# A second level of a seven-product scheme inside the first FFN product, for two pairs of neighbouring blocks

## The chip, the core and the metric

The kernel runs on one core of one Trainium2 chip. TensorE (PE) multiplies a stationary 128x128 operand, loaded by a weight load (PEld), with a moving operand and adds into PSUM banks of 128 partitions x 512 fp32; there are eight of them. VectorE (DVE), ScalarE (ACT) and GpSimd (POOL) work beside it, and each runs its own queue in order. SyncE (SP) issues plain loads; loads that add to what lies in the destination are issued by POOL. The metric is the time of one execution in microseconds (us).

## What is computed

The reference is two layers of FFN, mixer, FFN on 512 tokens with 1024 channels, all fp32, and a final norm. The change touches the FFN alone, which occurs four times:

```python
def swiglu(x, w_in, w_out):
    gu = x @ w_in                       # 512 x 1024 by 1024 x 5632
    g, u = jnp.split(gu, 2, axis=-1)    # gate and up, 2816 columns each
    return (jax.nn.silu(g) * u) @ w_out
...
x = x + 0.5 * swiglu(rms_norm(x, ffn1_norm[l]), ffn1_w_in[l], ffn1_w_out[l])
```

`x @ w_in` is the first product of the title, the product with `w_out` the second.

## The kernel before

**Numbers in two parts.** Every fp32 operand is split into a rounded high part and a rest, and a product is three matmuls: high by high, rest by high, high by rest. The stationary operand is a 128x128 tile of the activations, the moving one is 128x512 of the weights. The helper `run` (L367, L368, L370) issues all three.

**The first product.** The first 256 columns of gate and of up are done plainly (`plain`, tile `cl`). The other 2560 columns of each are done in five blocks (`NB = 5`) of 512 gate and 512 up columns. The activations are taken as 2x2 parts (256 tokens by 512 channels), the weights of a block as four parts of 512x512: a and b are the upper and lower channel halves of gate, c and d those of up. One block takes seven products, numbered 1 to 7 in the code, where a plain 2x2 product takes eight. Of the weights, product 1 takes -a, product 2 takes b, 5 takes c+d, 6 takes a+c+d, 3 takes a+b+c+d, 7 takes a+c, 4 takes d. The sums c+a and d+c are made by loads that add (`Raw.load`, L157), the further ones by DVE (`sum`, L191). Product 2 is the lower channel half of the first 256 tokens by b; only gate of those tokens uses it.

A part of the weights comes in two granules of 128x1024 (two channel tiles of 512 columns). Each is one item of a stream in the order in which products use them: load into one of nine `raw` buffers, high part by ACT into `whi` (L196, L198), rest by DVE into `wlo` (L203, L205). There are three `whi` and three `wlo` buffers, so an item is prepared while the two items ahead of it are multiplied, and its buffers come free when the third item back is done. An item of a product is 12 matmuls, a product 24. Up to eight items ahead are loaded.

**PSUM and what follows a product.** Products 1, 6, 7 and 4 go into the pair of banks `A`, 5 and 3 into `B`, 2 into `C`. 6, 7 and 4 add to what is in the banks, so partial sums are copied out between: `snap` (ACT, L601) copies a pair of banks to `sn`, and `less` (DVE, L606) subtracts such a copy from a later state. `gate` (ACT, L705) is the silu, `times` (DVE, L711) multiplies by up. The gated block is transposed by PE (`tr`, L624) in the next block, after that one's first product, and copied by ACT to `at` (L628).

**Order of a block:** 1, 5, 6, 2, 7, 3, 4. `snap` copies banks `A` after 6, product 2 then goes to other banks, and 7 adds to `A`. In the very first FFN's first block 2 comes second. The order of instructions on each engine is set by a scheduler from the program; a stretch at the start and one at the end are kept as written.

**The second product** is done by the same scheme over `at` (tile `o`).

Of the kernel before, what the change touches and what calls it, by code (L numbers as in the profile page):

```python
# [9 lines left out]
F32 = mybir.dt.float32  # L10
F32R = mybir.dt.float32r
# [84 lines left out]
def encoder_kernel(  # L96
# [32 lines left out]
    def pair(s="ps"):  # L129
        return [bank(s), bank(s)]  # L130
# [86 lines left out]
    def stage_items():  # L217
        items, st = [], 0

        def add(*a, **k):  # L220
            items.append(Item(*a, stage=st, **k))

        made = {}

        def strassen(s, name, idx, sizes, order, dma=False):
            r = made.setdefault((s, name("a"), idx), {}) if dma and len(order) < 7 and order[0] > 2 else {}
            for q, q2 in () if r else (("a", ""), ("b", ""), ("c", "a"), ("d", "c")):
                r[q] = [
                    Raw((s, name(q), idx, g), n, *[(s, name(z), idx, g) for z in q2]) for g, n in enumerate(sizes)
                ]  # L230
# [4 lines left out]
            for m in order:  # L235
                for g in range(len(sizes)):
                    a, b, c, d = [r[q][g] for q in "abcd"]
                    if m == 1:
                        add(a, neg=True)
                    elif m == 2:  # L240
                        add(b)
                    elif m == 3:
                        add(r["s"][g] if "s" in r else d, None if dma else b)
                    elif m == 4:
                        add(d2[g])
                    elif m == 5:
                        add(d, then=a.key if dma and order is not ORDER_W else None)
                    elif m == 6:
                        t = r["s"][g] if "s" in r else d
                        add(t, None if dma else a, then=b.key if dma else None)  # L250
                    else:
                        add(c)

        def out_sizes(c):
            return (1024, 512) if c == 0 else (1024, 1024)

        def ffn(s):
            first = not items
            for g in range(4):
                add(Raw((s, "cl", g)), parts=2 if first and g < 2 else 1, pieces=2 if first and g == 0 else 1)  # L260
            for j in range(NB):
                order = (1, 2, 5, 6, 7, 3, 4) if s == (0, 1) and j == 0 else (1, 5, 6, 2, 7, 3, 4)
                strassen(s, lambda q: q, j, (1024, 1024), order)
            for order in ((1,), (2,), (5, 6, 7, 3), (4,)):
                for c in range(3):
                    strassen(s, lambda q: "o" + q, c, out_sizes(c), order)

        for l in range(L):
            ffn((l, 1))
            st += 1  # L270
            s = (l, 0)
            two = (1024, 1024)
            for g in VG:
                add(Raw((s, "v", g)), kept=g == VG[0])
            for g in range(3):
                add(Raw((s, "up", g), UC * len(UK[g]), (s, "uq", g)))
            for g in range(2):
                add(Raw((s, "un", g)), minus=(s, "um", g))
            for g in range(8):
                add(Raw((s, "qk", g)))  # L280
            for i in range(2):
                add(Raw((s, "fp", i), 1024, (s, "fq", i)))
                add(Raw((s, "fq", i)), minus=(s, "fp", i))
            for i in range(2):
                strassen(s, lambda q: "g" + q, i, two, ORDER_0[0 : 2 - i], True)
            for g in range(2):
                add(Raw((s, "n", 0, g)))
            for i, order in ((0, (5,)), (1, (2,)), (0, (6,)), (1, (5,)), (0, (7, 3)), (1, (6,)), (0, (4,)), (1, (7, 4, 3))):
                strassen(s, lambda q: "g" + q, i, two, order, True)
# [3 lines left out]
            strassen(s, lambda q: "w" + q, 0, two, ORDER_W, True)  # L293
            ffn((l, 2))
        return items

# [75 lines left out]
    def split(hi, lo, src, scale=None):  # L372
        if scale is None:
            S.activation(hi, src, AF.Copy)
            return V.tensor_tensor(lo, src, hi.bitcast(F32), ALU.subtract)
        S.activation(hi, src, AF.Copy, scale=scale)
        return V.scalar_tensor_tensor(lo, src, scale, hi.bitcast(F32), ALU.mult, ALU.subtract)
# [220 lines left out]
    def snap(ps):  # L598
        t = slot(F32, "sn", (2, T))
        for b in range(2):  # L600
            S.activation(t[:, b, :], ps[b], AF.Copy)  # L601
        return t
# [5 lines left out]
    def stage_ffn(norm, nxt, late):  # L608
# [52 lines left out]
        first = norm.idx == 0  # L661
        if not first:
            norm.rstd()
        with tc.manual_schedule(engines={mybir.EngineType.DVE, mybir.EngineType.Activation}) if first else nullcontext():
            t1 = combo(b11, b11, b12, ALU.subtract, "t1")
            if first:
                norm.squares(0, 0)
            t3 = combo(b12, b12, b22, ALU.subtract, "t3")
            if first:
                norm.squares(0, 1)  # L670
            t2 = combo(b22, b22, b11, ALU.add, "t2")
            if first:
                norm.squares(1, 0)
            if first:
                ws.prep(ws.pos + 3)
            V.tensor_tensor(b21, b21, b22, ALU.subtract)
            t4 = (hx[0][:, :, 256:512], lx[0][:, :, 256:512])
            split(t4[0], t4[1], b21)
# [87 lines left out]
        def second(s1):  # L766
            pc = pair("C")
            product(pc, acts[2], K4, True)
            less(pc, s1)

        for jb in range(NB):
            f0 = 2 + 4 * jb
            if first and jb == 0:
                with tc.manual_schedule(engines={mybir.EngineType.DVE, mybir.EngineType.Activation}):
                    pa = pair("A")
# [1256 lines left out]
```

## Time and profile before

| | us |
|---|---|
| median of three runs (1870.36 to 1871.58) | 1871.33 |
| the profiled execution | 1870.75 |
| its span, first to last instruction | 1869.0 |
| PE busy | 1859.4 |
| DVE busy | 1492.2 |
| ACT busy | 1175.9 |
| POOL busy | 182.8 |

A row of a group or a timeline names line, engine, operation, output<-input and shape; in brackets or behind a bar stands how long the engine was idle before it and what it waited for. Matmuls overlap: each has a duration of its own, but the next starts before it ends, so the distance between starts is what a matmul takes of PE. The granted TensorE clock is 0.999 of full speed over the span.

### The profile page before, as it was taken

How to read it: one execution, taken by the hardware profiler on the slowest of the kernel's cores; microseconds unless marked ns; L12 is line 12 of the kernel's file. 1: busy time of each engine (PE TensorE's matmuls, PEld its weight loads, DVE VectorE, ACT ScalarE, POOL GpSimd, SP SyncE). 2: the span in 40 equal slices, each digit the busy share in tenths (PEclk: the TensorE clock that was granted, in tenths of full speed). 3: DMA queues.
4: the chain of work that ended last, by engine and by line, in shares of the span. 5: the costliest groups of instructions: out<-in, count | busy, mean ns of one | idle time of the engine just before them, and what ended most of it. 6: DMA issues, size and time to landing. Idle time of an engine off the chain costs nothing.

```text
span 1869.0 us, 25963 instructions
## 1 busy us (share of the span) xinstructions
PE 1859.4 (99%) x9609; PEld 1584.6 (85%) x9609; DVE 1492.2 (80%) x1831; ACT 1175.9 (63%) x1751; POOL 182.8 (10%) x219
## 2 busy tenths in 40 slices
PE   9999999999999999999999999999999999999998
PEld 7888888889998888888888888888899988888886
DVE  7777799758879777779977777997687797777898
ACT  6655565768656655566665556667676576555665
POOL 0101011100211001001000000101002110100010
PEclk9999999999999999999999999999999999999999
DMA  8777588864998477659757764979649985766595
GB/s 296 205 193 202 150 239 267 243 209 126 245 258 224 131 201 193 181 150 266 240 148 188 208 178 153 253 230 281 202 132 252 247 222 140 196 181 168 179 270 184
DMA packets 110319, 384.57 MB, mean 206 GB/s; under 512 B 12512, under 2 KB 12640, under 8 KB 110192
## 3 DMA queue, kind: packets, MB, share of 16 engines
q1 hardware_dynamic: 79952, 276.81, 42.1%
q0 software_dynamic: 29808, 105.32, 30.7%
q8 instruction: 75, 1.23, 0.3%
q10 hardware_dynamic: 432, 0.79, 0.1%
q14 instruction: 52, 0.43, 0.1%
HBM read 375.13 MB, written 6.29 MB: 204 GB/s over the span
## 4 chain that ended last, share of the span: by engine, by line
PE 97%; DVE 1%; ACT 0%; DMA 0%; issue 0%; DVEq 0%; ACTq 0%
PE A L367 9%; PE A L370 9%; PE A L368 9%; PE o L370 7%; PE o L367 7%; PE o L368 7%; PE B L367 5%; PE B L368 5%; PE B L370 5%; PE ps L367 3%; PE ps L368 3%; PE ps L370 3%; PE C L370 2%; PE C L368 2%; PE C L367 2%; PE tr L624 2%
## 5 line engine op out<-in xcount | busy, mean ns | idle before, releaser
L205 DVE TENSOR_TENSOR wlo<-raw,whi 128x1024 fp32r<-128x1024 f32 (+2 forms) x524 | 619.4, 1189 | 224.4 <-ACT whi L198 221.5
L198 ACT ACTIVATE whi<-raw 128x1024 fp32r<-128x1024 f32 (+2 forms) x524 | 537.5, 1032 | 341.6 <-PE A L368 134.1
L157 POOL DMA_DIRECT2D raw<-in_wst_dram x170 | 147.5, 871 | 1449.2 <-DMA raw<-in_wst_dram 826.1
L191 DVE TENSOR_TENSOR raw<-raw,raw 128x1024 f32<-128x1024 f32 (+1 forms) x128 | 151.4, 1188 | 2.4
L367 PE MATMUL A<-whi,xh 128*128 128x512 f32 x320 | 124.5, 389 | 0.0
L368 PE MATMUL A<-whi,xl 128*128 128x512 f32 x320 | 124.5, 389 | 0.0
L705 ACT ACTIVATE th<-sn,r 128x512 f32<-128x512 f32 x80 | 57.0, 715 | 73.7 <-DVE sn L606 73.7
L196 ACT ACTIVATE whi<-raw 128x1024 fp32r<-128x1024 f32 x76 | 78.7, 1036 | 35.3 <-issue 17.1
L203 DVE SCALAR_TENSOR_TENSOR wlo<-raw,whi 128x1024 fp32r<-128x1024 f32 x76 | 90.6, 1192 | 8.9 <-ACT whi L196 8.8
L370 PE MATMUL A<-wlo,xh 128*128 128x512 f32 x320 | 92.1, 389 | 0.0
L601 ACT ACTIVATE sn<-A 128x512 f32<-128x512 f32 x96 | 56.1, 590 | 45.9 <-PE A L370 45.9
L368 PEld LDWEIGHTS A<-whi,xl 128*128 128x128 f32 x320 | 60.1, 188 | 12.5
L370 PEld LDWEIGHTS A<-wlo,xh 128*128 128x128 f32 x320 | 60.1, 188 | 12.5
L367 PEld LDWEIGHTS A<-whi,xh 128*128 128x128 f32 x320 | 60.1, 188 | 12.5
L367 PE MATMUL B<-whi,t1h 128*128 128x512 f32 x160 | 63.7, 398 | 0.0
L367 PE MATMUL A<-whi,t2h 128*128 128x512 f32 x160 | 62.5, 391 | 0.0
L367 PE MATMUL B<-whi,xh 128*128 128x512 f32 x160 | 62.4, 390 | 0.0
L368 PE MATMUL B<-whi,xl 128*128 128x512 f32 x160 | 62.3, 390 | 0.0
L368 PE MATMUL B<-whi,t1l 128*128 128x512 f32 x160 | 62.3, 390 | 0.0
L368 PE MATMUL A<-whi,t2l 128*128 128x512 f32 x160 | 62.3, 389 | 0.0
L368 PE MATMUL A<-whi,t3l 128*128 128x512 f32 x160 | 62.2, 389 | 0.0
L367 PE MATMUL C<-whi,xh 128*128 128x512 f32 x160 | 62.2, 389 | 0.0
(454 smaller groups left out, 4897.5 us busy)
## 6 DMA issues: line engine op xcount, KB each, us to landing
raw<-in_wst_dram SPq DMA_DIRECT2D x463, 512.0 KB
raw<-in_wst_dram POOLq DMA_DIRECT2D x184, 512.0 KB, 8.0
raw<-in_wst_dram SPq DMA_DIRECT2D x28, 256.0 KB
vc<-vd SPq DMA_DIRECT2D x28, 256.0 KB
bm<-in_near_dram SPq DMA_DIRECT2D x16, 384.0 KB
vd<-v SPq DMA_DIRECT2D x8, 512.0 KB
dft<-in_dft_dram POOLq DMA_DIRECT2D x4, 514.0 KB, 10.0
x<-in_xin_dram SPq DMA_DIRECT2D x4, 512.0 KB
```

The source lines that it names most:

```text
L157: z = G.dma_start(out=self.t, in_=wst[GRAN_AT[plus]][:, 0 : self.n], accum_op=ALU.add)
L191: V.tensor_tensor(self.raw.t, self.raw.t, self.add.t, ALU.add)
L196: S.activation(self.out[0][:, cs], self.raw.t[:, cs], AF.Copy, scale=-1.0)
L198: S.activation(self.out[0][:, cs], self.raw.t[:, cs], AF.Copy)
L203: self.last = V.scalar_tensor_tensor(lo, t, -1.0, hi.bitcast(F32), ALU.mult, ALU.subtract)
L205: self.last = V.tensor_tensor(lo, t, hi.bitcast(F32), ALU.subtract)
L367: PE.matmul(ps, lh, rh, start=start, stop=False, skip_group_check=again)
L368: PE.matmul(ps, *((lh, rl) if w == "l" else (ll, rh)), start=False, stop=False, skip_group_check=again)
L370: PE.matmul(ps, *((ll, rh) if w == "l" else (lh, rl)), start=False, stop=stop, skip_group_check=again)
L601: S.activation(t[:, b, :], ps[b], AF.Copy)
L624: PE.transpose(tr[:, k, b * P : (b + 1) * P], a[:, b, (q + k) * P : (q + k + 1) * P], ident)
L705: S.activation(th[:, b, :], g[:, b, :], AF.Silu, scale=norm.r[:, c : c + 1])
```

## The change

Blocks 1 and 2, and blocks 3 and 4, are made pairs. Product 2 of both blocks of a pair has the same activations (256 tokens by 512 channels); their weights, b of the one and b of the other side by side, are 512 x 1024. This joined product is now done by the seven-product scheme once more, with parts of 128 tokens by 256 channels and 256 x 512. An inner part of the weights is then just one granule, and an inner product is one item and six matmuls (two channel tiles, three matmuls each, one bank). Block 0 keeps its product 2.

- `stage_items`: seven inner items take the place of the four items of two products 2. In the first block of a pair inner 1, 5, 2, 6 and 3 stand ahead of the outer products 5, 6, 7, 3 and 4; in the second block inner 7 and 4 stand ahead of 6 and 7. The inner weights are loaded apart from b of the outer product 3, which was shared with product 2 before and is now loaded for the sum of product 3 alone. Two of the inner items need a load that adds, two need a sum on DVE.
- `inner_parts` and `inner_split` make the inner activations once per FFN: four DVE operations of 128x256, and a split of 128x1024 on ACT and DVE. Three of the seven inner activations are slices of what is there.
- `pair_block` replaces the block's body: one bank `qA` lives through the pair, `qB` and `qC` through its first block; results are added into `s1` piece by piece, with one copy `sq` by ACT in the first block.

```diff
+ORDER_P = (1, 5, 6, 7, 3, 4)
+INNER = (((5, 1), (6, 5), (7, 2), (3, 6), (4, 3)), ((6, 7), (7, 4)))
+PAIRS = (1, 3)
...
             for j in range(NB):
-                order = (1, 2, 5, 6, 7, 3, 4) if s == (0, 1) and j == 0 else (1, 5, 6, 2, 7, 3, 4)
-                strassen(s, lambda q: q, j, (1024, 1024), order)
+                if not j:
+                    four(s, lambda q: q, j, (1024, 1024), ORDER_0 if first else ORDER_W)
+                    continue
+                if j in PAIRS:
+                    key = [[(s, "b", j + z, g) for g in range(2)] for z in range(2)]
+                    a, b, c = Raw(key[0][0]), Raw(key[0][1]), Raw(key[1][0], 1024, key[0][0])
+                    d, d2 = Raw(key[1][1], 1024, key[1][0]), Raw(key[1][1])
+                    parts = {1: (a, None, True), 2: (b,), 3: (d, b), 4: (d2,), 5: (d,), 6: (d, a), 7: (c,)}
+                inner = dict(INNER[j not in PAIRS])
+                for m in strassen(s, lambda q: q, j, (1024, 1024), ORDER_P):
+                    if m in inner:
+                        add(*parts[inner[m]])
...
+        def inner_parts(src):
+            y = [[src[:, 2 * i : 2 * i + 2, b * P : (b + 1) * P] for b in range(2)] for i in range(2)]
+            t = slot(F32, "v", (4, 2, P))
+            v = [t[:, z] for z in range(4)]
+            V.tensor_tensor(v[0], y[0][0], y[0][1], ALU.subtract)
...
+        def inner(ps, m, begin):
+            wh, wl = ws.next()
+            h, l = fine[m]
+            terms = []
+            for k in range(2):
+                z = slice(k * T, (k + 1) * T)
+                terms.append((ps, h[:, k], l[:, k], wh[:, z], wl[:, z], "r", begin and k == 0, k == 1))
+            run(terms, not begin)
...
+        def pair_block(jb, late_at):
+            one = jb in PAIRS
+            pa = pair("A")
+            product(pa, acts[1], K4, True)
+            s1 = snap(pa)
+            settle_at()
+            if one:
+                qa = kept["a"] = bank("qA")
+                inner(qa, 1, True)
+                V.tensor_tensor(s1[:, 0, :], qa, s1[:, 0, :], ALU.add)
...
+            product(pa, acts[6], K4, False, again=True)
+            s2 = snap(pa)
+            if one:
+                qc = bank("qC")
+                inner(qc, 2, True)
+                V.tensor_tensor(s1[:, 0, :], qc, s1[:, 0, :], ALU.subtract)
+            else:
+                inner(qa, 4, False)
+                V.tensor_tensor(s1[:, 0, :], qa, s1[:, 0, :], ALU.subtract)
+                z1 = gate(s1, 0)
+            product(pa, acts[7], K4, False, again=True)
...
+                if jb == 1:
+                    inner_split()
+                pair_block(jb, late_at)
```

Summed over the program, PE has 48 matmuls of 128x512 fewer (9620 to 9572). DVE has 24 `wlo` and 16 sums of 128x1024 more, 24 operations of 128x512 that read or finish an inner product more than it had for `C`, 16 of 128x256 and 4 splits. ACT has 24 `whi`, 8 copies `sq` and 4 splits more. SP issues 40 loads of 512 KB more, POOL 16 adding loads.

Three places, all in the first FFN's block 1. In these rows lines of the changed kernel are some 20 to 50 higher for the same code (L601 is L620, L606 is L625, L198 is L201, L205 is L208, L191 is L194); numbers behind a name only tell buffers apart.

ACT after product 6, before:

```order
L198 ACTIVATE whi_811<-raw_645 128x1024
L601 ACTIVATE sn_827<-A_684 128x512
L198 ACTIVATE whi_834<-raw_663 128x1024
L601 ACTIVATE sn_827<-A_685 128x512
L198 ACTIVATE whi_853<-raw_686 128x1024
L705 ACTIVATE th_872<-sn_722,r_515 128x512
```

ACT at the same place now:

```order
L201 ACTIVATE whi_832<-raw_669 128x1024
L842 ACTIVATE sq_828<-qB_817 128x512
L201 ACTIVATE whi_850<-raw_695 128x1024
L620 ACTIVATE sn_866<-A_693 128x512
L201 ACTIVATE whi_872<-raw_714 128x1024
L620 ACTIVATE sn_866<-A_694 128x512
L201 ACTIVATE whi_886<-raw_611 128x1024
```

The two copies of `A` and the `whi` between them keep their order; the copy `sq` comes ahead of them, and the silu of the first half moves to the block's end.

DVE from the items of product 6 to those of product 7, before:

```order
L205 TENSOR_TENSOR wlo_754<-raw_558,whi_753 128x1024
L191 TENSOR_TENSOR raw_558<-raw_558,raw_620 128x1024
L205 TENSOR_TENSOR wlo_773<-raw_566,whi_772 128x1024
L191 TENSOR_TENSOR raw_566<-raw_566,raw_645 128x1024
L205 TENSOR_TENSOR wlo_794<-raw_620,whi_793 128x1024
L205 TENSOR_TENSOR wlo_812<-raw_645,whi_811 128x1024
L205 TENSOR_TENSOR wlo_835<-raw_663,whi_834 128x1024
L205 TENSOR_TENSOR wlo_854<-raw_686,whi_853 128x1024
```

DVE from the end of inner 1 (`qA`) to product 7 now:

```order
L833 TENSOR_TENSOR sn_733<-qA_762,sn_733 128x512
L208 TENSOR_TENSOR wlo_779<-raw_611,whi_778 128x1024
L194 TENSOR_TENSOR raw_611<-raw_611,raw_563 128x1024
L208 TENSOR_TENSOR wlo_798<-raw_570,whi_797 128x1024
L194 TENSOR_TENSOR raw_570<-raw_570,raw_776 128x1024
L208 TENSOR_TENSOR wlo_819<-raw_590,whi_818 128x1024
L194 TENSOR_TENSOR raw_590<-raw_590,raw_795 128x1024
L208 TENSOR_TENSOR wlo_833<-raw_669,whi_832 128x1024
L208 TENSOR_TENSOR wlo_851<-raw_695,whi_850 128x1024
L208 TENSOR_TENSOR wlo_873<-raw_714,whi_872 128x1024
```

The sums for product 3 (`raw_776` and `raw_795` are b) still stand right behind the items of product 6; the sum for inner 6 (`raw_611`) and one inner item come between, and the sums now wait for a load of b that was there before for product 2.

PE where product 6 ends, before (the last two matmuls of 6, then product 2; its 24 matmuls run on to product 7):

```order
L370 MATMUL A_685<-wlo_773,t2h_336 128x512 x2
L367 MATMUL C_830<-whi_793,xh_136 128x512
L368 MATMUL C_830<-whi_793,xl_137 128x512
L367 MATMUL C_830<-whi_793,xh_136 128x512
L368 MATMUL C_830<-whi_793,xl_137 128x512
L367 MATMUL C_831<-whi_793,xh_136 128x512
```

PE there now (the last two of 6, the whole of inner 2, the first of 7):

```order
L389 MATMUL A_694<-wlo_819,t2h_336 128x512 x2
L386 MATMUL qC_869<-whi_832,xh_136 128x512
L387 MATMUL qC_869<-whi_832,xl_137 128x512
L386 MATMUL qC_869<-whi_832,xh_136 128x512
L387 MATMUL qC_869<-whi_832,xl_137 128x512
L389 MATMUL qC_869<-wlo_833,xh_136 128x512 x2
L386 MATMUL A_693<-whi_850,t3h_327 128x512
```

Between the last matmul of 6 into `A` and the first of 7 into the same banks there were 24 matmuls into `C`; now there are 6 into `qC` (or, in the second block of a pair, into `qA`).

More of the change, by code (lines that the diff above doesn't have):

```diff
@@ L252, in strassen, with four @@
                         add(c)
+        def four(*a):
+            for _ in strassen(*a):
+                pass
         def out_sizes(c):
@@ L284, in stage_items @@
             for i in range(2):
-                strassen(s, lambda q: "g" + q, i, two, ORDER_0[0 : 2 - i], True)
+                four(s, lambda q: "g" + q, i, two, ORDER_0[0 : 2 - i], True)
             for g in range(2):
@@ L288, in stage_items @@
             for i, order in ((0, (5,)), (1, (2,)), (0, (6,)), (1, (5,)), (0, (7, 3)), (1, (6,)), (0, (4,)), (1, (7, 4, 3))):
-                strassen(s, lambda q: "g" + q, i, two, order, True)
+                four(s, lambda q: "g" + q, i, two, order, True)
                 st += not i and order[0] == 5
@@ L292, in stage_items @@
                 add(Raw((s, "n", 1, g)))
-            strassen(s, lambda q: "w" + q, 0, two, ORDER_W, True)
+            four(s, lambda q: "w" + q, 0, two, ORDER_W, True)
             ffn((l, 2))
```

54 lines of the change are left out of this document (53 added, 1 removed).

## The prediction, made before the changed kernel was run

> **What bounds the kernel now.** I read the busy shares first, then the chain of waits.
>
> ```profile
> span 1869.0 us, 25963 instructions
> ...
> PE 1859.4 (99%) x9609; PEld 1584.6 (85%) x9609; DVE 1492.2 (80%) x1831; ACT 1175.9 (63%) x1751; POOL 182.8 (10%) x219
> ...
> PE 97%; DVE 1%; ACT 0%; DMA 0%; issue 0%; DVEq 0%; ACTq 0%
> ```
>
> PE is busy all but 9.6 us and makes 97% of the chain that ended last. A share is a mean over stages, so I asked for the stages that the change touches: the first FFN's blocks 2 and 3 (from one transpose of gated results to the next, see the third fence), and its second product.
>
> ```profile
> 108.90:148.80 39.90, 39.90 (x186) 33.28 (x185) 28.40 (x28) 22.56 (x29) 3.46 (x4) 1.00 0.68 183
> 148.80:188.60 39.80, 39.80 (x185) 33.19 (x184) 28.42 (x28) 22.60 (x31) 3.46 (x4) 1.00 0.70 184
> 234.00:326.00 92.00, 92.00 (x409) 76.20 (x408) 89.87 (x95) 57.18 (x71) 11.30 (x14) 1.00 0.85 252
> ```
>
> Behind the stretch and its length stand PE, PEld, DVE, ACT and POOL busy, the granted clock, the DMA share and GB/s. In a block PE never stops, DVE works 28.4 of 39.9 us and ACT 22.6. In the second product DVE is at 89.87 of 92 us, and PE still doesn't stop. So a matmul taken away shortens the kernel, as long as preparation, copies and loads keep up.
>
> **The matmuls.** The price is the distance of starts. From the timeline of PE, product 2 of block 2 and what follows, and from the chain, the transposes in blocks 2 and 3:
>
> ```profile
> 126.84 0.39 PE L367 MATMUL C<-whi,xh 128*128 128x512 f32 x1
> ...
> 132.28 0.39 PE L367 MATMUL A<-whi,t3h 128*128 128x512 f32 x1
> ```
>
> ```profile
> 114.36 1.75 PE tr L624 x16
> ...
> 154.21 1.75 PE tr L624 x16
> ```
>
> 24 matmuls take 132.28 - 126.84 = 5.44 us, 0.2267 each (the 0.39 is a latency that overlaps). A block is 7 x 5.44 + 1.75 = 39.83 us, and the transposes stand 39.85 apart: nothing else is in it. A pair now has 2 x 24 = 48 matmuls in products 2, and would have 7 x 6 = 42. Six fewer in 2 pairs x 4 FFNs make 48 x 0.2267 = **10.88 us**. The first block of a pair becomes 174 matmuls and 16 transposes, 41.2 us, the second 156, 37.1 us: 78.3 where two blocks take 79.7. [...] The trace's 0.2267 us, which fills the block to 0.02 us, decides here.
>
> **DVE and ACT.** Groups over block 2, and the 128x256 group of the whole run:
>
> ```profile
> L205 DVE TENSOR_TENSOR wlo<-raw,whi 128x1024 fp32r<-128x1024 f32 x12 | 14.7, 1225 | 9.1 <-ACT whi L198 9.1
> L198 ACT ACTIVATE whi<-raw 128x1024 fp32r<-128x1024 f32 x13 | 13.8, 1061 | 11.8 <-PE A L368 9.0 <-PE B L368 1.5 <-PE C L368 0.7
> ...
> L191 DVE TENSOR_TENSOR raw<-raw,raw 128x1024 f32<-128x1024 f32 x4 | 4.9, 1225 | 0.1
> ...
> L705 ACT ACTIVATE th<-sn,r 128x512 f32<-128x512 f32 x4 | 2.9, 716 | 4.1 <-DVE sn L606 4.1
> ...
> L601 ACT ACTIVATE sn<-A 128x512 f32<-128x512 f32 x4 | 2.4, 589 | 2.4 <-PE A L370 2.4
> ...
> L606 DVE TENSOR_TENSOR sn<-A,sn 128x512 f32<-128x512 f32 x2 | 1.4, 688 | 0.6 <-PE A L370 0.6
> ```
>
> ```profile
> L427 DVE TENSOR_SCALAR xr<-xt,xt 128x256 f32<-128x256 f32 x14 | 4.3, 349 | 0.0
> ```
>
> DVE waits for ACT, and ACT for PE to free a `whi` buffer: preparation is held back by PE, not the other way. Per pair DVE gets three more `wlo` (3 x 1.225), two sums (2 x 1.225) and three operations on 128x512 (seven for the inner products less four on `C`, 3 x 0.69): 8.2 us, beside 56.8 us of now, 65.0 of 78.3 us (83%). The first block bears most: three items, two sums, two on 128x512, 7.5 us, 35.9 of 41.2 us (87%). The second has the same count of items and one 0.69 more, 29.1 of 37.1 us. ACT gets 3 x 1.061 + 0.589 = 3.8 us per pair, 49 of 78.3. All of it lies beside PE. An inner item is only 1.36 us of matmuls against 1.225 of `wlo`, or 2.45 with a sum. But inner items stand singly between two granules of 2.72 us, and the sums run early, in DVE's gaps. Going through DVE's order of the first block with these durations and the three buffers (a `wlo` not before the third item back is done), each `wlo` ends some 2 us or more ahead of the matmul that reads it, the tightest in product 4 of the first block. I take 0 for it. A missed cover would show as PE waiting for `wlo`.
>
> The inner activations: four operations of 128x256 at 0.35 (the nearest row; up to 0.69, the row of twice the width), 1.4 us, in DVE's queue ahead of the last activation split at each FFN's start; and once 1.2 us on DVE and 1.06 on ACT in block 1. In the second FFN's start:
>
> ```profile
> 621.87 1.22 DVE L676 TENSOR_TENSOR xr<-xr,xr 128x1024 f32<-128x1024 f32 x1
> ...
> 624.27 1.23 DVE L375 TENSOR_TENSOR xl<-xr,xh 128x1024 fp32r<-128x1024 f32 x1 [1.19 <-ACT xh L374]
> ...
> 626.45 1.23 DVE L203 SCALAR_TENSOR_TENSOR wlo<-raw,whi 128x1024 fp32r<-128x1024 f32 x1 [0.95 <-ACT whi L196]
> ```
>
> ```profile
> 628.33 0.39 PE L367 MATMUL A<-whi,xh 128*128 128x512 f32 x1
> ```
>
> The queue has gaps of 1.19 and 0.95 us behind the insertion, and the `wlo` at 626.45 is the second granule of a product that starts at 628.33: needed at 628.33 + 2.72 + 0.91 = 632.0, ready 4.3 us earlier. 1.4 to 2.8 us late costs nothing there.
>
> **The copy ahead of product 7.** Product 7 writes banks that ACT still copies. Product 2's 5.44 us covered that; now an inner product's 1.36 us does. After product 6 of block 2, which ends at 126.84, ACT has:
>
> ```profile
> 125.68 0.60 ACT L601 ACTIVATE sn<-A 128x512 f32<-128x512 f32 x1 [1.21 <-PE A L370]
> 126.59 1.06 ACT L198 ACTIVATE whi<-raw 128x1024 fp32r<-128x1024 f32 x1 [0.31 <-PE A L368]
> 127.56 0.58 ACT L601 ACTIVATE sn<-A 128x512 f32<-128x512 f32 x1
> ```
>
> The second copy ends at 128.14, 1.30 us after product 6. Product 7's first four matmuls go to the first bank, so the second is touched 1.36 + 0.91 = 2.27 us after: 0.97 us in hand. In a pair's second block a silu half stands between the first copy and that `whi`, 0.72 us, of which 0.40 fall on ACT's idle 0.31 and the overlap: the copy is done some 0.3 us later, with 0.6 in hand. I take 0; the place comes 2 x 8 = 16 times.
>
> **The loads.** Over blocks 2 and 3 (79.7 us, 20 plain loads and 8 adding):
>
> ```profile
> q1 hardware_dynamic: 2880, 10.49, 38.6%
> q0 software_dynamic: 1113, 4.08, 29.9%
> ...
> raw<-in_wst_dram POOLq DMA_DIRECT2D x8, 512.0 KB, 7.9
> ```
>
> A plain load takes 0.386 x 79.7 / 20 = 1.54 us of all engines, an adding one 2.98. A pair will have 25 and 10: 68.3 of 78.3 us, 87%, where the second product lives with 85% and 252 GB/s. So the sum of bandwidth fits (234 GB/s). In order: SP issues a load when its buffer comes free. The shortest lead is b of product 3, whose buffer the sum for product 6 frees and whose own sum stands seven DVE operations later: six of about 1.15 us (their starts) and one of 0.69, 7.6 us. No row has a plain load's landing. The adding one's 7.9 us bounds it from above; 0.52 MB at the stretch's 184 GB/s, 2.8 us, is nearer, since a plain load occupies the engines half as long. Even at 7.9 DVE would wait 0.3 us, and the `wlo` behind it has 3.6 us in hand. 0.
>
> **Sum.** 10.88 us, nothing on the other side. The profiled execution of 1870.75 becomes 1859.9; the median stands 0.58 above that execution, so **1860.5** is what I forecast.
>
> **Rivals.** (1) *Slower: ACT loses the race ahead of product 7.* For it: cover falls from 5.44 to 1.36 us and ACT's queue is in order, so a `whi` that waits for its buffer or a silu that waits for DVE (4.1 us of such idle in the group above) holds the copy. Against it: 0.6 to 0.97 us in hand, and the silu that stands ahead is of the half that is ready earlier. Each us beyond that stops PE 16 times; at 0.68 us (1.3 to 1.65 late in all) the gain is gone. Late by two more ACT operations of 1.06, 2.1 less 0.8 in hand, it costs 21 us: about 1881. (2) *DVE falls behind in the first block of a pair.* For it: 87%, and waits now take 11 of 40 us, of which only 5.3 are left. Against it: those waits are for PE's buffers and shrink when DVE is late. If 0.7 us per pair are missing, 5.6 us come back: 1866. (3) *The loads of b come late.* For it: 87% of DMA, with adding loads between. Against it: 7.6 us of lead and 3.6 in hand. [...] Were DVE to stop 5 us in each first block, 1.4 would reach PE, 8 times: 11 us, so no change. (4) *The gain is real but given back in the second product,* since DVE, 98% busy there, may set that stage's end: arriving 2.72 us earlier in each FFN would then only make PE wait, about 1871. Against it: DVE enters that stage without arrears, for in block 4, which ends at 228.4,
>
> ```profile
> 220.52 1.23 DVE L205 TENSOR_TENSOR wlo<-raw,whi 128x1024 fp32r<-128x1024 f32 x1 [0.99 <-ACT whi L198]
> ```
>
> it still waits, and the changed block 4 leaves it some 7 us free.
>
> **Chances and range.** As forecast, 1859 to 1862: 0.78. Part of it lost by (2) or a smaller (1), 1862 to 1867: 0.08. No change by (3) or (4): 0.05. Slower by (1) or several of these: 0.09. A difference under 0.2% (3.7 us) can't be told from none here. Faster by more is the first and most of the second, 0.85; same 0.06; slower 0.09. Below, nothing but the noise of runs (0.6 us each way) adds to the removed matmuls; above, I go to 1866, where (2) ends.
>
> **What would show it.** PE 48 matmuls fewer; the transposes of a pair about 41.2 and 37.1 us apart; no idle time of PE ahead of `A`, `qA`, `qB`, `qC`; the second product starting 2.72 us earlier in each FFN. DVE busy 1492.2 + 8 x 8.2 + 4 x 2.6 = 1568, 84%; 56 loads, 29.4 MB more. Wrong would be PE waiting for `sn` by ACT (1), for `wlo` (2), DVE's sums waiting for `raw` (3), or PE idle in `o` (4).

## The result

The changed kernel takes 1859.76 us (1858.98 to 1860.66), the kernel before beside it 1871.45 (1870.36 to 1872.14): a ratio of 0.9938, 95% interval 0.9921 to 0.9955. The forecast was 1860.5 in a range of 1859 to 1866, and the likeliest case came in.

From the page of the changed kernel, the lines that answer to those shown of before:

```profile
span 1857.9 us, 26118 instructions
...
PE 1847.8 (99%) x9561; PEld 1574.3 (85%) x9561; DVE 1556.5 (84%) x1915; ACT 1203.1 (65%) x1787; POOL 196.8 (11%) x235
...
DMA packets 118384, 413.94 MB, mean 223 GB/s; under 512 B 13408, under 2 KB 13536, under 8 KB 118256
```

PE has 9561 matmuls instead of 9609, 48 fewer, and is busy 11.6 us less; the span is 11.1 us shorter. PE is idle 10.1 us, where it was 9.6. The chain of waits in the first FFN has the transposes that close each block of columns:

```profile
73.74 1.75 PE tr L643 x16
...
114.94 1.75 PE tr L643 x16
...
152.07 1.75 PE tr L643 x16
```

They stand 41.20 and 37.13 us apart: the first block of a pair and its second block. Both numbers were forecast. Busy times between them (stretch and length, then PE, PEld, DVE, ACT, POOL, the granted clock, DMA share and GB/s), for both blocks of the first pair and the first block of the second:

```profile
69.40:110.60 41.20, 41.20 (x192) 34.35 (x191) 36.52 (x38) 25.74 (x32) 4.33 (x5) 1.00 0.78 219
110.60:147.70 37.10, 37.10 (x174) 30.96 (x173) 28.54 (x30) 22.18 (x28) 4.32 (x5) 1.00 0.88 248
147.70:188.90 41.20, 41.20 (x192) 34.35 (x191) 35.08 (x36) 25.86 (x34) 4.06 (x6) 1.00 0.80 220
```

PE never stops in them. DVE is at 36.5 and 35.1 of 41.2 us in the first blocks. The race ahead of product 7 is in the timeline of ACT (`sn` of L620 is the second bank's copy), first in a first block, then in a second one:

```profile
88.68 1.06 ACT L201 ACTIVATE whi<-raw 128x1024 fp32r<-128x1024 f32 x1 [0.31 <-PE A L387]
89.65 0.58 ACT L620 ACTIVATE sn<-A 128x512 f32<-128x512 f32 x1
...
128.12 0.71 ACT L755 ACTIVATE th<-sn,r 128x512 f32<-128x512 f32 x1
128.73 1.05 ACT L201 ACTIVATE whi<-raw 128x1024 fp32r<-128x1024 f32 x1
129.68 0.59 ACT L620 ACTIVATE sn<-A 128x512 f32<-128x512 f32 x1
```

and PE's first matmuls of product 7 on the second bank in the two blocks:

```profile
91.20 0.39 PE L386 MATMUL A<-whi,t3h 128*128 128x512 f32 x1
...
131.05 0.39 PE L386 MATMUL A<-whi,t3h 128*128 128x512 f32 x1
```

The copies end at 90.23 and 130.27, so 0.97 and 0.78 us are in hand.

**Where the time went, by FFN.** From the start of the last `cl` row of PE's timeline (two matmuls) to that of the first `o` matmul lie the five blocks, and all kernels below are set beside each other so. The kernel before was run again beside each set of kernels, with medians from 1870.19 to 1871.45 us; each ratio is to the one beside it:

| kernel (label of its run) | FFN 1 | FFN 2 | FFN 3 | FFN 4 | median us | ratio to before, 95% interval |
|---|---|---|---|---|---|---|
| before | 198.92 | 198.82 | 198.82 | 198.83 | 1871.45 | |
| after | 196.40 | 196.11 | 196.10 | 196.11 | 1859.76 | 0.9938 (0.9921 to 0.9955) |
| e1_one_pair | 197.76 | 197.46 | 197.46 | 197.47 | 1866.04 | 0.9976 (0.9966 to 0.9986) |
| e2_six_back | 199.08 | 198.82 | 198.83 | 198.82 | 1870.29 | 0.9998 (0.9989 to 1.0007) |
| e6_last_only | 198.98 | 198.83 | 198.83 | 196.11 | 1868.66 | 0.9992 (0.9983 to 1.0000) |
| e6_first_three | 196.40 | 196.11 | 196.11 | 198.82 | 1862.70 | 0.9958 (0.9945 to 0.9970) |
| e8_no_cover | 199.08 | 198.84 | 198.84 | 198.84 | 1871.82 | 1.0005 (0.9996 to 1.0013) |
| e8_wlo_first | 196.76 | 196.48 | 196.49 | 196.49 | 1861.28 | 0.9950 (0.9938 to 0.9963) |
| e3_copy_plus1 | 199.36 | 199.06 | 199.25 | 199.10 | 1871.50 | 1.0009 (1.0000 to 1.0018) |
| e3_copy_plus3 | 205.53 | 205.23 | 208.45 | 206.88 | 1907.69 | 1.0207 (1.0193 to 1.0221) |
| e3_copy_in_four | 196.39 | 196.11 | 196.10 | 196.10 | 1860.29 | 0.9946 (0.9933 to 0.9960) |
| e4_dve_plus4 | 196.67 | 196.72 | 196.11 | 196.11 | 1860.43 | 0.9948 (0.9935 to 0.9960) |
| e4_dve_plus8 | 204.80 | 205.26 | 201.93 | 202.02 | 1891.08 | 1.0111 (1.0098 to 1.0125) |
| e9_loads_plus4 | 196.40 | 196.11 | 196.11 | 196.11 | 1860.73 | 0.9946 (0.9934 to 0.9959) |

Of the 11.1 us of span, 10.65 lie in these stretches (2.52 + 3 x 2.71). In the first FFN 0.20 us are missing in block 0 and the first product of block 1, which the change leaves alone: from the last `cl` row to the chain's first transposes it takes 45.34 us there instead of 45.14. Most of that, 0.17, lies beside PE's early transposes, which the new schedule has in other places. The rest of the span's difference is outside of the stretches: 1.0 us less up to the first FFN's last `cl` row, 1.0 more behind the last FFN's first `o`, and half a us less between the first two FFNs. The lengths at the two ends differ by as much between the kernels below, also where nothing in them is changed (see the last FFN, below), and I don't count them as the change's.

### The profile page after: what moved, and what is told of

It reads as the page before. It is cut to its first block, busy times and chain, and to the rows that moved or that the text cites. A ratio compares the mean times of both kernels' runs of the same rounds, so it can differ in the third digit from the quotient of the medians.

```text
span 1857.9 us, 26118 instructions
## 1 busy us (share of the span) xinstructions
PE 1847.8 (99%) x9561; PEld 1574.3 (85%) x9561; DVE 1556.5 (84%) x1915; ACT 1203.1 (65%) x1787; POOL 196.8 (11%) x235
## 2 busy tenths in 40 slices
DMA packets 118384, 413.94 MB, mean 223 GB/s; under 512 B 13408, under 2 KB 13536, under 8 KB 118256
## 3 DMA queue, kind: packets, MB, share of 16 engines
q8 instruction: 75, 1.23, 0.3%
## 4 chain that ended last, share of the span: by engine, by line
PE 97%; DMA 1%; DVE 1%; issue 0%; ACT 0%; POOL 0%; ACTq 0%; DVEq 0%; SPq 0%; POOLq 0%
PE A L386 9%; PE A L389 9%; PE A L387 9%; PE o L389 7%; PE o L386 7%; PE o L387 7%; PE B L386 5%; PE B L387 5%; PE B L389 5%; PE ps L386 3%; PE ps L387 3%; PE ps L389 3%; PE tr L643 2%; PE cl L387 2%; PE cl L389 2%; PE cl L386 2%
## 5 line engine op out<-in xcount | busy, mean ns | idle before, releaser
L208 DVE TENSOR_TENSOR wlo<-raw,whi 128x1024 fp32r<-128x1024 f32 (+1 forms) x540 | 638.7, 1191 | 170.3 <-ACT whi L201 169.3
L201 ACT ACTIVATE whi<-raw 128x1024 fp32r<-128x1024 f32 (+1 forms) x540 | 555.2, 1034 | 317.8 <-PE A L387 89.7
L160 POOL DMA_DIRECT2D raw<-in_wst_dram x186 | 161.4, 873 | 1458.9 <-DMA raw<-in_wst_dram 766.5
L194 DVE TENSOR_TENSOR raw<-raw,raw 128x1024 f32<-128x1024 f32 (+1 forms) x144 | 171.2, 1193 | 2.7
L199 ACT ACTIVATE whi<-raw 128x1024 fp32r<-128x1024 f32 x84 | 87.1, 1037 | 42.1 <-issue 21.5
L206 DVE SCALAR_TENSOR_TENSOR wlo<-raw,whi 128x1024 fp32r<-128x1024 f32 x84 | 99.8, 1196 | 4.6 <-ACT whi L199 4.5
L620 ACT ACTIVATE sn<-A 128x512 f32<-128x512 f32 x96 | 56.2, 591 | 46.4 <-PE A L389 46.4
L386 PE MATMUL A<-whi,t3h 128*128 128x512 f32 x160 | 62.2, 389 | 0.0
```

Source lines behind the costliest of these rows:

```text
L160: z = G.dma_start(out=self.t, in_=wst[GRAN_AT[plus]][:, 0 : self.n], accum_op=ALU.add)
L194: V.tensor_tensor(self.raw.t, self.raw.t, self.add.t, ALU.add)
L199: S.activation(self.out[0][:, cs], self.raw.t[:, cs], AF.Copy, scale=-1.0)
L201: S.activation(self.out[0][:, cs], self.raw.t[:, cs], AF.Copy)
L206: self.last = V.scalar_tensor_tensor(lo, t, -1.0, hi.bitcast(F32), ALU.mult, ALU.subtract)
L208: self.last = V.tensor_tensor(lo, t, hi.bitcast(F32), ALU.subtract)
```

## The experiments

The theory is the prediction's: PE sets the time, a matmul costs its distance of starts, and preparation, copies and loads have something in hand. The rivals are its four.

**Half of the change.** One pair instead of two:

```diff
-PAIRS = (1, 3)
+PAIRS = (1,)
...
-                if not j:
+                if j not in (1, 2):
...
-            if jb:
+            if jb in (1, 2):
```

> Only blocks 1 and 2 are joined; blocks 3 and 4 are done as in the kernel before. Theory (PE sets the time, a matmul costs 0.2267 us, all else is covered): 24 of the 48 matmuls are back, 5.44 us, so the change of 11.69 us becomes some 6.2 us: 1871.45 - 5.44 = 1866.0, and 1865.2 if the measured 1859.76 + 5.44 is taken. Rival: the gain comes from somewhere else (an earlier start, other order of DVE's or ACT's work at the start of a FFN, where the four operations for the inner activations stand): then one pair would bring all of it, 1860, or none, 1871. The transposes of blocks 1 and 2 stand 41.2 and 37.1 us apart, those of blocks 3 and 4 39.85.

Measured 1866.04 us. Each of the last three FFNs gained 1.36 us, half of 2.71. Its chain of waits in the first FFN:

```profile
73.87 1.75 PE tr L643 x16
...
115.07 1.75 PE tr L643 x16
...
152.20 1.75 PE tr L643 x16
...
192.05 1.75 PE tr L643 x16
```

41.20, 37.13 and, for block 3 as it was, 39.85 us. The gain lies in the pairs, in proportion to their number, and nothing of it comes from the FFN's start, where the inner activations are made in this kernel too. (In this kernel and in e6_last_only the blocks of the first FFN that are no longer joined take the weights of products 2, 5 and 6 in another order than their code multiplies them, so their values are others; matmuls, loads and copies are as many.)

**The six matmuls given back.** The inner product into `qB` is done twice:

```diff
+            if m == 5:
+                run(terms, not begin)
             run(terms, not begin)
```

> Each pair does its inner product into qB twice, with the same weights: 6 matmuls more per pair, 48 in the kernel, and nothing else changed. Theory: 48 x 0.2267 = 10.88 us come back, 1859.76 + 10.88 = 1870.6, as the kernel before; the first block of a pair becomes 42.56 us. [...] If DVE, ACT or the loads set the pace in the pairs, the added PE work would be covered: 1860.

Measured 1870.29, no different from before, and 10.5 us above the changed kernel. In the chain:

```profile
73.71 1.75 PE tr L643 x16
...
116.27 1.75 PE tr L643 x16
...
153.40 1.75 PE tr L643 x16
```

The first block is 42.56 us, 1.36 more than with six matmuls fewer: 0.227 each. All else of the change is still in this kernel, its DVE operations, sums, copies and loads, and it costs nothing: FFNs 2 to 4 take 198.82 us as before, and the first 0.16 more, which are those of block 0 told above.

**Rival (4), the second product.** The change in the last FFN alone, and in all but the last:

```diff
-                if not j:
+                if not j or s != (1, 2):
...
-            if jb:
+            if jb and late:
```

> Only the last FFN joins products 2; the three others are as before. Theory: 12 matmuls fewer, 2.72 us: 1871.45 - 2.72 = 1868.7. Rival (4) for this one FFN: its second product gives 1.1 us back, as the profile after shows there (PE waits for wlo), so the change brings 1.6 us: 1869.8. In the profile: from the last matmul of the closing block of columns to the first of the second product 195.9 us instead of 198.6, and in the second product PE idle for 1.1 us or not.

> Only the first three FFNs join products 2, the last is as before. Theory: 36 matmuls fewer, 8.16 us: 1870.55 - 8.16 = 1862.4. Rival (4) in the last FFN's second product (there the change gives 1.1 us back): the three bring 8.2 and the fourth only 1.6, so this kernel would be only 1.6 us above the changed one, 1861.4. In the profile: from the first matmul of the last second product to the end 114.2 us, as before, where the changed kernel has 115.2; if it is 115 to 116 here too, with the last FFN unchanged, this length varies by execution and the change doesn't set it.

Measured 1868.66 and 1862.70. The first is 1.9 to 2.8 us below before, depending on which median of it is taken (1870.55 beside this run, 1871.45 beside the changed kernel), the second 7.5 to 8.8 (1870.21 and 1871.45). The stretches are sharper: 2.71 to 2.72 us where a FFN is changed (2.52 in the first), at most 0.06 elsewhere. For the first three FFNs rival (4) is settled by PE's starts. Counted from the first `o` matmul, the first 400 of some 460 starts of each second product agree with those of the kernel before to 0.002 us, in every kernel of the table. For the last FFN the end of the span has to do. What lies behind the last FFN's first `o` matmul, of the kernel before, the changed one, e6_last_only and e6_first_three:

```profile
1754.82:1869.00 114.18, 106.82 (x479) 88.15 (x477) 106.45 (x129) 69.95 (x91) 13.07 (x15) 0.99 0.77 226
```

```profile
1742.69:1857.90 115.21, 107.56 (x479) 88.00 (x477) 106.72 (x129) 70.21 (x91) 13.10 (x15) 0.99 0.78 223
```

```profile
1750.82:1867.10 116.28, 107.52 (x479) 88.00 (x477) 106.72 (x129) 69.96 (x91) 13.04 (x15) 0.98 0.76 222
```

```profile
1746.65:1861.90 115.25, 107.25 (x479) 88.14 (x477) 106.69 (x129) 69.93 (x91) 13.04 (x15) 0.98 0.77 224
```

The kernel whose last FFN is unchanged has 115.25 us here, as the changed one, against 114.18 of before. The length varies by 2.1 us between the profiled kernels, and not with the arrival: e8_no_cover (below), which comes to this place as late as before, has 116.3, and e2_six_back, as late, 115.1. In the changed kernel PE waits there once for `wlo`, 0.27 us, a sign that the prediction had named for (4); but e2_six_back has the same wait of 0.26. So this us is not given back by an earlier arrival, and rival (4) falls. What makes the length vary stays open.

**Rival (1), the cover ahead of product 7.** First the cover is taken away: the inner product between products 6 and 7 goes behind 7, with PE's order held.

```diff
-INNER = (((5, 1), (6, 5), (7, 2), (3, 6), (4, 3)), ((6, 7), (7, 4)))
+INNER = (((5, 1), (6, 5), (3, 2), (13, 6), (4, 3)), ((6, 7), (3, 4)))
...
-                    if m in inner:
-                        add(*parts[inner[m]])
+                    for q in (m, 10 + m):
+                        if q in inner:
+                            add(*parts[inner[q]])
...
+            fixed = tc.manual_schedule(engines={mybir.EngineType.PE})
+            fixed.__enter__()
             pa = pair("A")
...
+            product(pa, acts[7], K4, False, again=True)
+            less(pa, sb)
             if one:
                 qc = bank("qC")
                 inner(qc, 2, True)
...
-            product(pa, acts[7], K4, False, again=True)
-            less(pa, sb)
...
+            fixed.__exit__(None, None, None)
             times(z1, pa, 0)
```

> The inner product that stands between product 6 and product 7 (qC in a pair's first block, qA in the second) is moved behind product 7, PE's order otherwise held as it was: product 7 follows product 6 at once. Theory (the copy of the second bank ends 1.30 us after product 6, product 7 touches that bank after its first four matmuls, 0.91 us): PE stops 0.39 us at 16 places, 6.2 us, 1866.0, with PE waiting for sn by ACT; the silu that stood ahead of the copy in the second block stands later too, so both blocks lose the same. Rival: the copy is fast enough or the wait is caught up elsewhere, 1859.8. Rival the other way: ACT falls behind for good, over 1870.

Measured 1871.82: the whole gain is gone, 12 us where 6.2 were expected. The waits of PE, and then its timeline in a first block (the fourth matmul of product 7 and the fifth, which goes to the second bank) and in a second one:

```profile
PE A L387 <- ACT sn L621: 5.9, 16, 0.5
```

```profile
89.51 0.39 PE L388 MATMUL A<-whi,t3l 128*128 128x512 f32 x1
90.17 0.50 PE L387 MATMUL A<-whi,t3h 128*128 128x512 f32 x1 [0.27 <-ACT sn L621]
90.51 0.40 PE L388 MATMUL A<-whi,t3l 128*128 128x512 f32 x1
...
129.92 0.39 PE L388 MATMUL A<-whi,t3l 128*128 128x512 f32 x1
130.78 0.50 PE L387 MATMUL A<-whi,t3h 128*128 128x512 f32 x1 [0.46 <-ACT sn L621]
```

```profile
89.54 0.58 ACT L621 ACTIVATE sn<-A 128x512 f32<-128x512 f32 x1
...
130.14 0.58 ACT L621 ACTIVATE sn<-A 128x512 f32<-128x512 f32 x1
```

The copies end at 90.12 and 130.72; the fifth matmul was due at 89.74 and 130.15. In the first block it is late by 0.38, as worked out (0.39). In the second it is late by 0.57, since a silu still stands ahead of the copy: it isn't the one that moved. And each wait costs more than that: the matmul starts 0.05 to 0.06 us after the copy's end, the next one follows after 0.34 us instead of 0.227, and some 0.03 are lost right behind. Product 7's first granule takes 3.29 and 3.51 us instead of 2.72, so 0.57 and 0.79, and 8 x (0.57 + 0.79) = 10.9 us, which is what the four stretches show (2.7 each).

To see that it is this wait and not the inner product's new place, the same kernel with another order of matmuls inside product 7, as the scheduler sets it when PE isn't held:

```diff
-            fixed = tc.manual_schedule(engines={mybir.EngineType.PE})
-            fixed.__enter__()
...
-            fixed.__exit__(None, None, None)
```

> As the run without cover (the inner product stands behind product 7), but with PE's order inside product 7 changed: in a first block the two wlo matmuls of the first bank come ahead of the second bank's first matmul, 0.45 us more, in a second block these two and one of the next granule, 0.68 us more; ACT's and DVE's orders are the same as without cover. Theory: there the second bank was wanted 0.38 us (first block) and 0.57 us (second) before its copy was done; 0.45 and 0.68 cover both: no wait, 1860. Rival (what cost 12 us there was not this wait but the inner product's new place): 1871.8 again.

Measured 1861.28. The wait is gone but for a trace. In the first block 0.45 us just meets the copy:

```profile
89.79 0.61 PE L390 MATMUL A<-wlo,t3h 128*128 128x512 f32 x2
90.25 0.48 PE L387 MATMUL A<-whi,t3h 128*128 128x512 f32 x1
90.56 0.40 PE L388 MATMUL A<-whi,t3l 128*128 128x512 f32 x1
```

It starts on time and the next follows after 0.31 us instead of 0.227. In the second blocks, where 0.68 us stand ahead, the next one follows after some 0.29; the stretches are 0.36 to 0.39 us longer than the changed kernel's.

Then the margin from the other side: copies added behind the second one, with the inner product in its place and PE's order held (here with n = 1 and n = 3).

```diff
             s2 = snap(pa)
+            for _ in range(n):
+                S.activation(s2[:, 1, :], pa[1], AF.Copy)
```

> ACT copies the second bank of product 6 once more (one added copy of 128x512, 0.48 us from start to start, in each of the 16 blocks of pairs), PE's and DVE's order as they were. Theory: the copy is done 1.30 us after product 6 in a first block and some 0.3 later in a second one, with 0.97 and 0.6 us in hand; 0.48 fits into both: 1859.8, no wait of PE. Rival (1), no margin: 16 x 0.48 = 7.7 us, 1867.5.

> The same with three added copies, 1.44 us. Theory: in a first block 1.44 - 0.97 = 0.47 us late; in a second block a silu of 0.65 us now stands between the copies, so 1.44 + 0.65 - 0.6 to 0.9 = 1.2 to 1.5 late; 8 x 0.47 + 8 x 1.35 = 14.6 us (12 to 16): 1874. PE waits for sn ahead of product 7's second bank. Rival (ACT's order lets it catch up, or PE's queue hides it): 1860. Rival (no margin at all): 16 x 1.44 + 8 x 0.65 = 28 us, 1888.

Measured 1871.50 and 1907.69: both expectations missed. The timeline of ACT with one added copy (L854) says why:

```profile
89.74 0.58 ACT L620 ACTIVATE sn<-A 128x512 f32<-128x512 f32 x1
90.22 1.05 ACT L201 ACTIVATE whi<-raw 128x1024 fp32r<-128x1024 f32 x1
91.17 0.58 ACT L854 ACTIVATE sn<-A 128x512 f32<-128x512 f32 x1
```

A `whi` stands between. The bank is free at 91.75 instead of 90.32, 1.43 us later and not 0.48. With 0.97 in hand that is 0.46 us late, in a second block 1.43 - 0.78 = 0.65. By the price of a wait found above, 0.2 more each: 8 x (0.66 + 0.85) = 12.1 us; the stretches show 12.05. In the kernel without cover a mean of 0.48 us late cost 10.9, the whole gain.

With three, the first blocks are 1.71 us late and the second ones 2.45. Two waits as the timeline of PE has them:

```profile
93.81 0.50 PE L386 MATMUL A<-whi,t3h 128*128 128x512 f32 x1 [1.60 <-ACT sn L854]
...
136.32 0.50 PE L386 MATMUL A<-whi,t3h 128*128 128x512 f32 x1 [2.35 <-ACT sn L854]
```

Product 7's first granule is 1.91 and 2.64 us longer, 36.4 us in all. The stretches are 41.4 us longer; the other 5 are told at the end.

Last, the margin with nothing between: the second copy in four pieces.

```diff
-            s2 = snap(pa)
+            s2 = slot(F32, "sn", (2, T))
+            S.activation(s2[:, 0, :], pa[0], AF.Copy)
+            for z in range(4):
+                c = slice(z * 128, (z + 1) * 128)
+                S.activation(s2[:, 1, c], pa[1][:, c], AF.Copy)
```

> The margin of the copy ahead of product 7, asked again with nothing between: the copy of product 6's second bank is made in four pieces of 128x128 directly one behind the other, in all 16 blocks of pairs; all other orders are as in the changed kernel. A 128x256 copy is 0.33 us and a 128x512 one 0.59 (0.48 from start to start), so the four should take some 0.9 to 1.0 us and end 0.35 to 0.45 us later. Theory (0.97 us in hand in a first block, and 0.78 in a second one, as the added copy, which came 1.43 us later and made PE wait from 0.46 and 0.65 us late, shows): no wait, 1860. Rival (1), no margin: 16 x (0.4 + 0.2 for the restart) = 10 us, 1870.

Measured 1860.29, with every stretch as in the changed kernel.

```profile
90.46 0.76 ACT L855 ACTIVATE sn<-A 128x128 f32<-128x128 f32 x4
```

The four took 0.76 us, 0.18 more than the one copy instead of 0.4. So this shows no more than that 0.18 us fit; the margin of 0.97 and 0.78 rests on the copy that came 1.43 us later.

**Rival (2), DVE in the first block.** Four or eight operations of 128x1024 added at four places (here n = 1 and n = 2 at each), PE's order held (with eight, 15 matmuls around the end of product 4 of each first block still stand a few places elsewhere):

```diff
+                for _ in range(n):
+                    V.tensor_tensor(sb, sb, sb, ALU.max)
```

> Four added DVE operations of 128x1024 (1.225 us each, 4.9 us, in SBUF) in the first block of each pair, PE's order as it was. DVE was busy 36.5 and 35.1 of 41.2 us in the two first blocks of the first FFN and becomes busy 41.4 and 40.0. Theory (DVE has some 5 us left there): 0 to 2 us, 1860 to 1862, PE not idle or hardly. Rival (2), DVE is already behind and each of its operations ends on PE's path: 8 x 4.9 = 39 us, 1899.

> The same with eight added operations, 9.8 us: DVE would need 46.3 and 44.9 of 41.2 us. Theory: 5.1 and 3.7 us over in the first block, of which the preparation's lead of some 2 us is used up first; 8 x (4.4 - 2) = 19 to 8 x 4.4 = 35 us slower: 1879 to 1895, PE waiting for wlo in product 7, 3 and 4 of the first blocks. Rival, the second block's 8 us take up all of it: 1860 to 1862. Rival, no margin: 78 us, 1938.

Measured 1860.43 and 1891.08, both inside what the theory gave. The pair's two blocks with four, and with eight:

```profile
69.40:110.60 41.20, 41.20 (x191) 34.37 (x190) 40.27 (x42) 25.62 (x32) 3.46 (x4) 1.00 0.77 205
110.60:147.70 37.10, 37.10 (x172) 30.64 (x172) 28.35 (x30) 22.05 (x28) 4.32 (x5) 1.00 0.95 260
```

```profile
69.40:110.60 41.20, 40.09 (x185) 32.93 (x184) 40.27 (x40) 23.88 (x30) 3.77 (x5) 1.00 0.66 175
110.60:147.70 37.10, 35.16 (x157) 28.81 (x156) 28.18 (x29) 20.74 (x28) 4.32 (x5) 0.95 0.91 252
```

With four, DVE is at 40.27 of 41.2 us and PE doesn't stop here (the stretches of the first two FFNs are 0.3 and 0.6 us longer, those of the others not). With eight it is at the same 40.27, and now PE stops. The second block has room, but DVE can't make up its arrears there without PE seeing them:

```profile
PE B L386 <- ACT at L647: 10.9, 8, 2.3
PE B L389 <- DVE wlo L208: 8.9, 8, 1.1
```

The `wlo` waits are in product 3 of the first blocks. The others are at the start of the second blocks, and they name ACT. What ACT waited for there is in its timeline:

```profile
116.89 1.06 ACT L201 ACTIVATE whi<-raw 128x1024 fp32r<-128x1024 f32 x1 [2.74 <-DMA raw<-in_wst_dram]
...
120.24 1.06 ACT L201 ACTIVATE whi<-raw 128x1024 fp32r<-128x1024 f32 x1 [1.80 <-DMA raw<-in_wst_dram]
```

The two loads are adding ones. POOL issued them at 104.75 and 107.33, where the changed kernel issues the same two at 98.01 and 103.92, and they landed 12.0 and 12.8 us later instead of 9.4 and 9.8. Behind such a `whi` ACT's queue holds the copies for which PE waits. That POOL issues late because late `wlo` and sums free the `raw` buffers late is likely, but was not shown for these two.

**Rival (3), the loads.** Four plain loads of 512 KB more in each first block:

```diff
                 inner(qa, 1, True)
+                jk = slot(F32, "jk", (1024,))
+                nc.sync.dma_start(out=jk, in_=wst[GRAN_AT[((0, 1), "b", jb, 0)]])
...
                 inner(qb, 5, True)
+                nc.sync.dma_start(out=jk, in_=wst[GRAN_AT[((0, 1), "b", jb, 0)]])
...
                 inner(qc, 2, True)
+                nc.sync.dma_start(out=jk, in_=wst[GRAN_AT[((0, 1), "b", jb, 0)]])
...
                 inner(qa, 6, False)
+                nc.sync.dma_start(out=jk, in_=wst[GRAN_AT[((0, 1), "b", jb, 0)]])
```

> Four added plain loads of 512 KB (one behind each inner product's place in a pair's first block, 32 in all, 16.8 MB), into a buffer that nothing reads; PE's, DVE's and ACT's orders as they were. By the row of before an added load takes the engines 1.54 us, 6.2 us per pair: the DMA share of a pair goes from 0.83 and 0.76 (pairs of the first FFN after the change) to some 0.91 and 0.84. Theory (loads have lead in hand): 0, 1860, PE idle as before. Rival (3), loads on their limit: each first block is held by 1.5 us or more, of which the lead hides none, 8 x 1.5 to 8 x 6 = 12 to 49 us, DVE's sums waiting for raw.

Measured 1860.73, each stretch as in the changed kernel, with the two pairs' first blocks at

```profile
69.40:110.60 41.20, 41.20 (x191) 34.37 (x191) 36.72 (x37) 25.72 (x33) 3.46 (x4) 1.00 0.93 265
...
147.70:188.90 41.20, 41.20 (x192) 34.38 (x191) 35.00 (x35) 25.84 (x35) 4.43 (x6) 1.00 0.95 276
```

A DMA share of 0.93 and 0.95, and PE, DVE and ACT are as busy as without the loads. Rival (3) falls. None of these kernels beats the changed one.

## Why the prediction was right

- **The matmuls.** 10.88 us were forecast. The three later FFNs gained 2.71 each, the number of the sum to 0.01; the first 2.52. The first misses 0.20, which lie in blocks that the change leaves alone and which no term had. e1, e2 and the two e6 kernels show that the gain goes with the number of matmuls.
- **DVE and ACT at 0.** A pair was put at 65.0 us of DVE and measured 65.06 (the first one); the first block at 35.9, measured 36.5 and 35.1; ACT at 49, measured 47.9. The lead of `wlo` was worked out right, too: the tightest of the first pair's first block ends at 105.23 and is first read by product 4 at 107.52, 2.3 us later, where some 2 us were forecast; the others of that block have 2.9 us or more. The reserve of 5.3 us in a first block was right: 4.9 us more cost 0.3 and 0.6 us in the first two FFNs and nothing in the others, 9.8 us cost 31 in all. What the prediction said of rival (2), that missing time comes back on PE, held only beyond that reserve, and over half of the waits shown (10.9 of 19.8 us) came by way of loads and ACT's queue and not by `wlo`. DVE's total was put at 1568 and is 1556.5, with the 84 operations that were counted: by their own durations DVE's operations take 78.5 us more, where 76 were summed, but neighbours overlap in the record (the operation at 97.72 starts 0.09 us before the `wlo` of 1.23 us at 96.58 ends), and the busy time counts that once. Nothing hung on it.
- **The inner activations at 0.** Held: the second to fourth FFN lose nothing against six matmuls fewer per pair.
- **The copy ahead of product 7 at 0.** Held, and the margins too: 0.97 was forecast and measured in first blocks, 0.6 forecast and 0.78 measured in second ones. Wrong was the price beyond them. Rival (1) said that 0.68 us of lateness undoes the gain; a wait cost 0.2 us more than it was late, so 0.48 us did. The cover was needed in the order that PE has: without it the gain is gone. With two or three matmuls put ahead of the second bank's first one, it is nearly not needed.
- **The loads at 0.** Held, with more in hand than thought: the share of the first pair is 0.78 and 0.88, together 83% instead of 87%, and 0.95 still stops nobody. The 29.4 MB came as counted (413.94 against 384.57 MB).
- **Rival (4)** was put down to DVE's missing arrears. That held: in the first three FFNs the second product runs alike in every kernel, however early it starts, and the length of the end doesn't go with the arrival.

The forecast time stood 0.7 us above the measured one, about the 0.6 that the prediction allowed for the noise of runs. That it came so near is in part luck: the medians are 11.69 us apart, of which 10.65 lie in the stretches that the change touches. With the medians that the kernel before had beside the other kernels (1870.19 to 1870.55) the difference is 10.4 to 10.8.

## What to carry to other kernels

Where a trace shows the bounding engine filled to 0.02 us per block, the distance of starts times the number of instructions removed is the gain, and the work is in showing that each helper keeps its margin; work out each margin as the time at which the bank is touched less the time at which the copy ends. Before adding work to a helper, look at what its queue puts ahead of it: one operation that slipped in front turned 0.48 us into 1.43. An engine busy for 85 to 89% of a stage of 41 us took 4.9 us more for nothing and not 9.8, and what then was late showed up two engines away.

## What the runs showed of the hardware

**A short wait of PE cost 0.2 us more than its lateness:** in e8_no_cover 0.57 us where the copy was 0.38 late, and 0.79 where it was 0.57 late. The list of waits shows about half of the loss: 5.9 us in 16 waits, where 10.9 were lost. The shown idle time begins at the end of a matmul's 0.39 us, 0.16 after the next one was due, and the slower restart isn't in it.

**Behind some waits of about two us the granted clock was halved.** In e3_copy_plus3 it drops to 0.50 for 3.41 us after three of the eight waits of 2.35 us and after none of those of 1.60; in e4_dve_plus8 it does so after two waits at a second block's start (the first of them is 1.94 us long). In the drop that begins at 1163.21 matmuls start 0.42 to 0.43 us apart instead of 0.227. By its length and clock a drop costs 1.7 us (an estimate: half of 3.41), and three times 1.7 are the 5 us that were open above. Two of the waits of 2.35 us, which end at 1161.71 and at 1769.23, each in two stretches: the first holds most of the wait, the second is the 3.41 us behind it (behind the stretch and its length stands PE busy; the granted clock is the third number from the end):

```profile
1159.79:1163.21 3.42, 1.50 (x7) 1.24 (x8) 1.13 (x1) 2.10 (x5) 0.00 (x0) 1.00 0.90 242
1163.21:1166.62 3.41, 3.41 (x10) 2.67 (x9) 1.22 (x1) 0.79 (x1) 0.00 (x0) 0.50 0.33 124
...
1767.37:1770.78 3.41, 1.55 (x7) 1.29 (x8) 1.07 (x1) 2.09 (x4) 0.00 (x0) 1.00 0.83 231
1770.78:1774.19 3.41, 3.41 (x17) 2.83 (x16) 1.97 (x3) 1.29 (x2) 0.00 (x0) 1.00 0.37 138
```

Behind the first wait the clock falls from 1.00 to 0.50, 1.50 us after the wait's end; behind the second it stays at 1.00. Why three of these waits had a drop behind them and five had none was not shown. That the other runs of this kernel took up to 8 us longer than the profiled one would need some five more such drops (an estimate, at 1.7 us each); it was not seen in a trace.
